# Expert-choice routing: logits in column groups of TensorE, and another place for the first weight splits

## The chip, the cores and the metric

The kernel runs on one core of a Trainium2 chip. The metric is device time of one execution in microseconds; for the kernel before, three runs were taken and their median is 1884.99 us. The core's engines are TensorE (PE, with its weight loads PEld), VectorE (DVE), ScalarE (ACT), GpSimd (POOL) and SyncE (SP), which issues most DMAs. Each engine works through its own queue in program order.

## The reference

Two layers over 1024 tokens of width 1024. Each has a mixer (layer 0: gated DeltaNet beside pooling; layer 1: a short gated convolution) with an output projection, then an expert-choice mixture of 16 experts, each of which takes the 128 tokens with the highest affinity for it. What matters here:

```
hl2 = modulate(rms_norm(xl, norm_ffn[i]), sh2_l, sc2_l)
xl = xl + g2_l[:, None] * expert_choice_ffn(hl2, router[i], w_gate[i], w_up[i], w_down[i])

def expert_choice_ffn(h, router, w_gate, w_up, w_down):
    aff = jax.nn.softmax(jnp.einsum('bnd,de->bne', h, router).astype(jnp.float32), axis=-1)
    gate, idx = lax.top_k(aff.transpose(0, 2, 1), cap)
    xg = h[bidx, idx]
    hid = jax.nn.silu(jnp.einsum('becd,edf->becf', xg, w_gate)) * jnp.einsum('becd,edf->becf', xg, w_up)
    y = jnp.einsum('becf,efd->becd', hid, w_down) * gate[..., None].astype(h.dtype)
    return jnp.zeros_like(h).at[bidx, idx].add(y)
```

## The kernel before

Large matmuls are made of three products of split operands: a float32 weight `raw` becomes `whi` (rounded to fp32r by a cast on ScalarE, L88) and `wlo` (the remainder, a subtraction at L89 on VectorE, or on GpSimd where `lo_engine` says so). Activations are split in the same way (`mh` and `ml`, `xh` and `xl`). L140 to L142 are the three products.

The output projection (`po`) goes over eight tiles of 128 tokens. As soon as half of a tile's 1024 columns is there, `route_half` transposes its four blocks (L262, `pt`), copies them (L264, `x2T`) and adds four matmuls to the tile's logits (L267, `lg`): the 128x128 block stands in the array, the router's 16 columns move through it. fp32 matmuls show as two records each, so a half has eight. `route_tile` then scales the logits (L277, `sml`), takes the softmax (L280, `sme`), transposes it into `v` (L291), and writes the modulated tile `h` and its affinities to the `table` in DRAM (L302). For tiles marked `late`, `h` is made in three steps: ScalarE's scaling (L296), then a multiplication by `a2` and an addition of `sh2` on GpSimd (L297, L300).

`select` finds the threshold of each expert by ten rounds of counting (`junk`, `cnt`, L315) with a chain of small operations between VectorE and TensorE, and then the place of each token (`before`, the tile `aff` in the rows of L356). The scratch of `select` lies in memory that the routing's pool held. `gather` turns places into indices: eight signs of 128x128 (`oh`; for the first expert four on ScalarE, L372, and four on VectorE, L370), summed on TensorE (`pi`, L373), cast to `idx` (L376), and an indirect DMA on GpSimd fetches the rows `xg` (L378). `transposed` makes `xh` and `xl` of them, and the expert's matmuls `gu` begin.

Each expert's weights are six granules of 1 MB (`granules`), which `fetch` loads into `raw` buffers, of which there are eight in the experts, and `prefetch` splits ahead of use. Up to six are split ahead. In `start0` and `start1`, four (layer 0) and six (layer 1) granules are fetched during the routing, two (layer 0) and one (layer 1) of them are split there by GpSimd and the cast, and each such split is followed by a further fetch. The rest of the six is split in `experts`: up to three on GpSimd after the last `routed` operation, the others on VectorE after `placed`, the last operation of `select`. `issue_after` sets such an order; otherwise the Tile scheduler sets it from the program and its priorities.

## Time and profile before

| what | us |
|---|---|
| runs | 1885.58, 1884.99, 1876.78 |
| profiled execution | 1877.14 |
| its span | 1875.4 |
| TensorE busy | 1667.6 (89%) |
| VectorE busy | 1288.0 (69%) |
| ScalarE busy | 898.3 (48%) |
| GpSimd busy | 518.9 (28%) |
| DMA, mean | 237 GB/s |

The span is the time from the first to the last instruction of the core, and the profiled execution is that of the rows below. A busy time says how long an engine had work in it, whether or not anything waited for it. The first routing ends near 697 us, its selection runs from 700 to 728 us, and layer 0's experts follow until some 1045 us; the second routing lies between 1376 and 1481 us, its selection ends at 1508, and the experts follow until some 1840 us.

### The profile page before, as it was taken

Reading aid. Unit: us, or ns where it says so; the run is one execution under the profiler, and the core shown is the slowest. Engines: PE = TensorE matmul, PEld = TensorE weight load, DVE = VectorE, ACT = ScalarE, POOL = GpSimd, SP = SyncE. Lnnn points to the kernel's source line nnn. Section 1 sums busy time; section 2 is a strip of 40 time slices with the busy share of each in tenths; the row PEclk is TensorE's granted clock in tenths of the full one; section 3 lists DMA queues with packets and bytes.
Section 4 is the critical chain, followed back from the end, with each engine's and each line's share of the span. In section 5 each row is a group of like instructions: output and inputs, shape, how many; then the busy total and the mean of one; then the engine's idle time right before and its main releaser. Section 6 shows DMA issues by size and latency. Waiting matters only on the chain. (4 is left out here: it accounts for less than half of the span.)

```text
span 1875.4 us, 26089 instructions
## 1 busy us (share of the span) xinstructions
PE 1667.6 (89%) x9581; PEld 1356.4 (72%) x9581; DVE 1288.0 (69%) x1964; ACT 898.3 (48%) x1568; POOL 518.9 (28%) x551
## 2 busy tenths in 40 slices
PE   5999998779979984999899899999999569999985
PEld 2998875667877773777678677888888457787774
DVE  4628685657778875789887768433545558889876
ACT  3635332433742444778766451111132367777753
POOL 4310296471431164222121261000012502211202
PEclk7989998879989985999999899999999779999998
DMA  7417665559586966899999648423264459999985
GB/s 289 146 35 228 214 203 136 158 155 280 168 295 203 386 248 211 303 341 368 363 368 324 205 131 295 163 68 109 82 222 146 175 194 330 356 373 365 362 277 190
DMA packets 261397, 443.71 MB, mean 237 GB/s; under 512 B 46521, under 2 KB 108714, under 8 KB 257174
## 3 DMA queue, kind: packets, MB, share of 16 engines
q1 hardware_dynamic: 252198, 408.76, 63.0%
q0 software_dynamic: 9072, 33.30, 7.0%
q8 instruction: 75, 1.23, 0.3%
q14 instruction: 52, 0.43, 0.1%
HBM read 368.65 MB, written 73.35 MB: 236 GB/s over the span
## 5 line engine op out<-in xcount | busy, mean ns | idle before, releaser
L89 DVE TENSOR_TENSOR wlo<-raw,whi 128x2048 fp32r<-128x2048 f32 (+3 forms) x247 | 476.4, 1960 | 91.5 <-ACT whi L88 91.4
L88 ACT CAST whi<-raw 128x2048 fp32r<-128x2048 f32 (+3 forms) x271 | 420.4, 1597 | 206.1 <-PE pin L141 67.6
L140 PE MATMUL gu<-whi,xh 128*128 128x512 f32 x512 | 207.4, 408 | 16.1 <-ACT whi L88 13.2
L141 PE MATMUL gu<-wlo,xh 128*128 128x512 f32 x512 | 207.9, 407 | 9.4 <-DVE wlo L89 9.3
L142 PE MATMUL gu<-whi,xl 128*128 128x512 f32 x512 | 204.8, 403 | 0.9 <-DVE xl L135 0.8
L484 POOL DMA_INDIRECT acc<-y,idx x31 | 72.5, 2338 | 364.6 <-DVE y L479 364.1
L141 PE MATMUL pin<-h1T,whi 128*128 128x512 f32 x384 | 149.8, 391 | 0.0
L142 PE MATMUL pin<-h1T,wlo 128*128 128x512 f32 x384 | 149.7, 392 | 0.0
L140 PE MATMUL pin<-h1T,whi 128*128 128x512 f32 x384 | 147.8, 393 | 0.0
L140 PEld LDWEIGHTS gu<-whi,xh 128*128 128x128 f32 x512 | 98.9, 194 | 42.8 <-ACT whi L88 17.5
L141 PEld LDWEIGHTS gu<-wlo,xh 128*128 128x128 f32 x512 | 98.8, 193 | 35.0 <-DVE wlo L89 12.7
L89 POOL TENSOR_TENSOR wlo<-raw,whi 128x1024 fp32r<-128x1024 f32 (+2 forms) x24 | 71.8, 3005 | 166.1 <-ACT whi L88 166.0
L142 PEld LDWEIGHTS gu<-whi,xl 128*128 128x128 f32 x512 | 98.3, 192 | 23.6 <-DVE xl L135 1.5
L810 DVE SCALAR_TENSOR_TENSOR adsum<-raw,cs,adsum 128x512 f32<-128x512 f32 (+1 forms) x77 | 95.1, 1235 | 23.5 <-DMA raw<-in_ada_w_dram 22.7
L474 PE MATMUL py<-whi,hh 128*128 128x512 f32 x256 | 106.4, 417 | 5.4 <-ACT hh L134 5.3
L474 PE MATMUL py<-wlo,hh 128*128 128x512 f32 x256 | 105.3, 411 | 0.1
L140 PE MATMUL pq<-hT,whi 128*128 128x512 f32 (+1 forms) x256 | 98.9, 386 | 3.3 <-DVE cv L1098 2.1
L378 POOL DMA_INDIRECT xg<-table,idx x32 | 49.2, 1539 | 181.3 <-ACT idx L376 148.4
L142 PE MATMUL pq<-hT,wlo 128*128 128x512 f32 (+1 forms) x256 | 98.4, 384 | 0.0
L141 PE MATMUL pq<-hT,whi 128*128 128x512 f32 (+1 forms) x256 | 98.2, 383 | 0.0
L141 PE MATMUL po<-wlo,mh 128*128 128x512 f32 x224 | 90.4, 404 | 4.7 <-DVE wlo L89 4.7
L140 PE MATMUL po<-whi,mh 128*128 128x512 f32 x224 | 90.5, 405 | 0.0
(397 smaller groups left out, 3739.1 us busy)
## 6 DMA issues: line engine op xcount, KB each, us to landing
raw<-in_w_gate_dram SPq DMA_DIRECT2D x64, 1024.0 KB
raw<-in_w_up_dram SPq DMA_DIRECT2D x64, 1024.0 KB
raw<-in_w_down_dram SPq DMA_DIRECT2D x64, 1024.0 KB
raw<-in_ada_w_dram SPq DMA_DIRECT2D x32, 1024.0 KB
raw<-in_ada_w_dram SPq DMA_DIRECT2D x64, 256.0 KB
raw<-in_sc_w_in_dram SPq DMA_DIRECT2D x12, 1024.0 KB
table<-h SPq DMA_DIRECT2D x16, 520.0 KB
raw<-in_ev_w_in_dram SPq DMA_DIRECT2D x16, 512.0 KB
```

The costliest lines, as they stand in the source:

```text
L88: nc.scalar.copy(hi[:, part], raw[:, part])
L89: (lo_engine or e).tensor_sub(lo[:, part], raw[:, part], hi[:, part])
L140: nc.tensor.matmul(out, lhs[0], rhs[0], start=start, stop=False)
L141: nc.tensor.matmul(out, lhs[0], rhs[1], start=False, stop=False)
L142: nc.tensor.matmul(out, lhs[1], rhs[0], start=False, stop=stop)
L378: nc.gpsimd.indirect_dma_start(out=xg, out_offset=None, in_=self.table[:, :], in_offset=bass.IndirectOffsetOnAxis(ap=idx, axis=0))
L474: nc.tensor.matmul(py, hh[:, k, :], g[w][:, k, :], start=k == w == 0, stop=False)
L484: self.scattered = nc.gpsimd.indirect_dma_start(out=self.acc[:, :], out_offset=bass.IndirectOffsetOnAxis(ap=idx, axis=0), in_=y, in_offset ...
L810: nc.vector.scalar_tensor_tensor(st["sum"], raw, cs[:, k, 0:1], st["sum"], op0=ALU.mult, op1=ALU.add)
```

## The change

The router's scaled columns are padded from 16 to 32 and stand in the array now, in four groups of 32 columns (`tile_position`), one for each block of 128 columns of the half; the 128 tokens move through all four. The logits come out transposed and in four partial sums on four groups of 32 partitions. When both halves are in, ScalarE copies the 128x128 partials (`lgp`) and a matmul with `fold`, a constant of four stacked identities, sums the groups and turns them back (L281 of the changed kernel). The early splits in the routing are gone, with the fetch behind each. The first round of the selection reads the constant `cand0` in place of a copy. And of the six splits ahead of the first expert, two are on GpSimd and four on VectorE, these after the last sign that VectorE makes for the first gather.

```diff
@@ -198,6 +198,11 @@
     for i, by in enumerate((-7 / 8, -1.0)):
         nc.vector.memset(co.down[:, i : i + 1], by / P)
 
+    co.fold = c.tile([P, NE], F32, name="fold")
+    nc.vector.tensor_tensor(co.fold, co.ident[:, 0:NE], co.ident[:, 32 : 32 + NE], op=ALU.add)
+    for i in (2, 3):
+        nc.vector.tensor_tensor(co.fold, co.fold, co.ident[:, 32 * i : 32 * i + NE], op=ALU.add)
+
     co.tri16 = c.tile([P, P], BF16, name="tri16")
     nc.gpsimd.memset(co.tri16, 1.0)
     nc.gpsimd.affine_select(
@@ -242,9 +247,11 @@
         nc.tensor.transpose(pt[:, : 2 * KD], rows, co.ident[: 2 * KD, : 2 * KD])
         cols = pool.tile([P, 2, KD, 1], F32, name=co.name("mod_cols"))
         nc.vector.tensor_copy(cols.rearrange("p s k o -> p (s k o)"), pt[:, : 2 * KD])
-        self.router = pool.tile([P, KD, NE], F32, name=co.name("router_a"))
+
+        self.router = pool.tile([P, KD, 32], F32, name=co.name("router_a"))
+        nc.gpsimd.memset(self.router, 0.0)
         shifts = pool.tile([P, KD, NE], F32, name=co.name("router_sh"))
-        for dst, i in ((shifts, 0), (self.router, 1)):
+        for dst, i in ((shifts, 0), (self.router[:, :, :NE], 1)):
             nc.vector.tensor_tensor(dst, w, cols[:, i].to_broadcast([P, KD, NE]), op=ALU.mult)
         pb = ps.tile([P, 512], F32, tag="y", name=co.name("pbias"))
         for k in range(KD):
@@ -262,13 +269,20 @@
             nc.tensor.transpose(pt[:, k * P : (k + 1) * P], x[:, (4 * half + k) * P : (4 * half + k + 1) * P], co.ident)
         xT = pool.tile([P, 4, P], F32, tag="x2T", name=co.name("x2T"), bufs=3)
         (nc.vector.tensor_copy if half else nc.scalar.copy)(xT.rearrange("p k t -> p (k t)"), pt)
+
         for k in range(4):
-            kk = 4 * half + k
-            nc.tensor.matmul(self.logits[:, :NE], xT[:, k, :], self.router[:, kk, :], start=kk == 0, stop=kk == KD - 1)
+            sl = slice(32 * k, 32 * k + 32)
+            nc.tensor.matmul(
+                self.logits[sl, :P], self.router[:, 4 * half + k, :], xT[:, k, :], start=half == 0, stop=half == 1, tile_position=(0, 32 * k),
+            )
+        if half:
+            parts = pool.tile([P, P], F32, tag="lgp", name=co.name("lgp"), bufs=1)
+            nc.scalar.copy(parts, self.logits[:, :P])
+            nc.tensor.matmul(self.logits[:, P : P + NE], parts, co.fold, start=True, stop=True)
 
     def route_tile(self, t, x, pool, ps, late=False):
 
-        co, nc, lg = self.co, self.nc, self.logits
+        co, nc, lg = self.co, self.nc, self.logits[:, P:]
         nc.sync.dma_start(self.acc[t * P : (t + 1) * P, :], x)
         r = co.rstd(pool, x, D, pool.tile([P, D], BF16, tag="h2j", name=co.name("h2j"), bufs=1))
 
@@ -298,7 +312,7 @@
             else:
                 nc.vector.scalar_tensor_tensor(h[:, :D], x, r, self.a2, op0=ALU.mult, op1=ALU.mult)
         self.routed = nc.gpsimd.tensor_tensor(h[:, :D], h[:, :D], self.sh2, op=ALU.add).ins
-        nc.scalar.copy(h[:, D:], e[:, 0, :])
+        self.weighed = nc.scalar.copy(h[:, D:], e[:, 0, :]).ins
         nc.sync.dma_start(self.table[t * P : (t + 1) * P, :], h)
 
     def select(self, pool, ps):
@@ -306,14 +320,13 @@
         co, nc, aff = self.co, self.nc, self.aff
         junk = pool.tile([P, SEQ], BF16, tag="junk", name=co.name("junk"), bufs=1)
         cand = pool.tile([P, 1], I32, tag="cand", name=co.name("cand"), bufs=1)
-        nc.vector.tensor_copy(cand, co.cand0)
         cnt = pool.tile([P, 1], F32, tag="cnt", name=co.name("cnt"), bufs=1)
         ok = pool.tile([P, 1], BF16, tag="ok", name=co.name("ok"), bufs=1)
         delta = pool.tile([P, 1], I32, tag="delta", name=co.name("delta"), bufs=1)
         for r in range(10):
-            step = 2.0 ** (27 - 3 * r)
+            step, old = 2.0 ** (27 - 3 * r), cand if r else co.cand0
             nc.vector.tensor_scalar(
-                junk, self.v, cand.bitcast(F32), 0.0, op0=ALU.is_ge, op1=ALU.add, accum_out=cnt
+                junk, self.v, old.bitcast(F32), 0.0, op0=ALU.is_ge, op1=ALU.add, accum_out=cnt
             )
             nc.vector.tensor_scalar(ok, cnt, float(CAP), None, op0=ALU.is_ge)
             pn = ps.tile([P, 512], F32, tag="tr", name=co.name("pn"))
@@ -321,7 +334,7 @@
             nc.tensor.matmul(pn[:, :1], co.same, ok, start=False, stop=True)
             if r < 7:
 
-                nc.vector.scalar_tensor_tensor(cand, pn[:, :1], step, cand, op0=ALU.mult, op1=ALU.add)
+                nc.vector.scalar_tensor_tensor(cand, pn[:, :1], step, old, op0=ALU.mult, op1=ALU.add)
             else:
                 nc.vector.tensor_scalar(delta, pn[:, :1], step, None, op0=ALU.mult)
                 nc.vector.tensor_tensor(cand, cand, delta, op=ALU.add)
@@ -353,9 +366,9 @@
 
         self.before = aff
         flat = lambda t: t.rearrange("p t e -> p (t e)")
-        self.placed = nc.vector.scalar_tensor_tensor(
+        nc.vector.scalar_tensor_tensor(
             flat(self.before), pp[:, : NT * NE], -1.0, flat(equal), op0=ALU.mult, op1=ALU.subtract
-        ).ins
+        )
 
     def gather(self, e, pool, ps, shared=False):
 
@@ -367,7 +380,7 @@
             before, vector = self.before[:, t, e : e + 1], int(shared and t % 2)
             if vector:
 
-                nc.vector.tensor_scalar(oh[:, t, :], co.places, before, 0.0, op0=ALU.add, op1=ALU.is_gt)
+                self.shared = nc.vector.tensor_scalar(oh[:, t, :], co.places, before, 0.0, op0=ALU.add, op1=ALU.is_gt).ins
             else:
                 nc.scalar.activation(oh[:, t, :], co.places, AF.Sign, bias=before)
             nc.tensor.matmul(pi[:, :1], oh[:, t, :], co.ones16[:, vector : vector + 1], start=t == 0, stop=t == NT - 1)
@@ -433,10 +446,10 @@
             with co.tc.issue_after(self.numbered):
                 rows.append(self.gather(e, pool, ps))
         ahead = self.transposed(rows[0][2], pool, ps)
-        with co.tc.issue_after(self.routed):
-            self.prefetch(weights, min(3, 6 - len(self.ahead)), nc.gpsimd)
-        with co.tc.issue_after(self.placed):
-            self.prefetch(weights, 6 - len(self.ahead), nc.vector)
+        with co.tc.issue_after(self.routed), co.tc.issue_after(self.weighed):
+            self.prefetch(weights, 2, nc.gpsimd)
+            with co.tc.issue_after(self.shared):
+                self.prefetch(weights, 4, nc.vector)
         for e in range(NE):
             (idx, aff, _), halves = rows.pop(0), ahead
             if e + 3 < NE:
@@ -1781,7 +1794,7 @@
 
     def start0(make, wpb, pool, ps, _):
         moe = make()
-        early = Weights(co, raws, Cycle(*((p, 1) for p in wpb)))
+        early = Weights(co, raws, wpa)
         ada = ada_steps(1, 0, pool, raws, ps, "tr")
         x_pool = Cycle((Bufs(out_pool, 3), 3), (Bufs(pool, 2), 2))
         for i, (t, srcs) in enumerate(pass2.items()):
@@ -1789,9 +1802,6 @@
                 step()
             if i == 4:
                 moe.fetch(early, 4)
-            if i in (5, 6):
-                moe.prefetch(early, 1, nc.gpsimd)
-                moe.fetch(early, 1)
             for step in out_project(
                 co, t, lambda: split_tile(co, out_pool, srcs), ws, part, out_pool, ps,
                 lambda t, x, late=i > 5: moe.route_tile(t, x, pool, ps, late), lambda t, x, nh: moe.route_half(t, x, nh, pool, ps), x_pool=x_pool,
@@ -1848,9 +1858,6 @@
         for i, steps in enumerate(tiles):
             if i == 1:
                 moe[0].fetch(weights, 6)
-            if i == 4:
-                moe[0].prefetch(weights, 1, nc.gpsimd)
-                moe[0].fetch(weights, 1)
             for step in steps:
                 step()
         return moe[0]
```

The order of VectorE at the end of layer 0's selection, before (`equal` and `aff` are its last two operations, `oh` the signs, `xl` the low half of the first expert's rows):

```order
L356 SCALAR_TENSOR_TENSOR aff_6918<-pp_7760,equal_7780 128x128
L89 TENSOR_TENSOR wlo_7891<-raw_7480,whi_7890 128x2048
L370 TENSOR_SCALAR oh_7788<-places,aff_6918 128x128 x4
L135 TENSOR_TENSOR xl_7866<-pt_7860,xh_7865 128x512
L135 TENSOR_TENSOR xl_7875<-pt_7869,xh_7874 128x512
L89 TENSOR_TENSOR wlo_8075<-raw_8072,whi_8074 128x2048
```

and with the change:

```order
L369 SCALAR_TENSOR_TENSOR aff_6923<-pp_7772,equal_7792 128x128
L383 TENSOR_SCALAR oh_7800<-places,aff_6923 128x128 x4
L89 TENSOR_TENSOR wlo_7899<-raw_7311,whi_7898 128x2048
L89 TENSOR_TENSOR wlo_7903<-raw_7313,whi_7902 128x2048
L89 TENSOR_TENSOR wlo_7909<-raw_7906,whi_7908 128x2048
L89 TENSOR_TENSOR wlo_7915<-raw_7912,whi_7914 128x2048
L135 TENSOR_TENSOR xl_7878<-pt_7872,xh_7877 128x512
```

The signs have moved ahead of the splits, and there are four splits where there was one.

The order of ScalarE from the last tile of layer 0's routing to the first signs, before:

```order
L296 ACTIVATE h_7648<-ox_7576,rstd_7631 128x1024
L292 COPY aff_6918<-sme_7639 128x16
L301 COPY h_7648<-sme_7639 128x16
L88 CAST whi_7886<-raw_7388 128x2048
L88 CAST whi_7890<-raw_7480 128x2048
L372 ACTIVATE oh_7788<-places,aff_6918 128x128 x4
L376 ACTIVATE idx_7806<-pi_7789 128x1
```

and with the change:

```order
L310 ACTIVATE h_7661<-ox_7586,rstd_7644 128x1024
L306 COPY aff_6923<-sme_7652 128x16
L315 COPY h_7661<-sme_7652 128x16
L88 CAST whi_7890<-raw_7307 128x2048
L88 CAST whi_7894<-raw_7309 128x2048
L88 CAST whi_7908<-raw_7906 128x2048
L88 CAST whi_7914<-raw_7912 128x2048
L88 CAST whi_7898<-raw_7311 128x2048
L88 CAST whi_7902<-raw_7313 128x2048
L385 ACTIVATE oh_7800<-places,aff_6923 128x128 x4
L389 ACTIVATE idx_7818<-pi_7801 128x1
```

Six casts, in place of two, stand between the last tile and the signs.

The order of GpSimd at the same place (L300 and L314 are the addition of `sh2`, L297 and L311 the multiplication by `a2`), before:

```order
L300 TENSOR_TENSOR h_7377<-h_7377,bc_6890 128x1024
L156 TENSOR_TENSOR rstd_7631<-rstd_7631,mhalf 128x1
L300 TENSOR_TENSOR h_7469<-h_7469,bc_6890 128x1024
L297 TENSOR_TENSOR h_7562<-h_7562,bc_6888 128x1024
L297 TENSOR_TENSOR h_7648<-h_7648,bc_6888 128x1024
L300 TENSOR_TENSOR h_7562<-h_7562,bc_6890 128x1024
L300 TENSOR_TENSOR h_7648<-h_7648,bc_6890 128x1024
L89 TENSOR_TENSOR wlo_7879<-raw_7294,whi_7878 128x2048
L89 TENSOR_TENSOR wlo_7883<-raw_7296,whi_7882 128x2048
L89 TENSOR_TENSOR wlo_7887<-raw_7388,whi_7886 128x2048
```

and with the change:

```order
L314 TENSOR_TENSOR h_7397<-h_7397,bc_6894 128x1024
L314 TENSOR_TENSOR h_7484<-h_7484,bc_6894 128x1024
L156 TENSOR_TENSOR rstd_7644<-rstd_7644,mhalf 128x1
L311 TENSOR_TENSOR h_7572<-h_7572,bc_6892 128x1024
L314 TENSOR_TENSOR h_7572<-h_7572,bc_6894 128x1024
L311 TENSOR_TENSOR h_7661<-h_7661,bc_6892 128x1024
L314 TENSOR_TENSOR h_7661<-h_7661,bc_6894 128x1024
L89 TENSOR_TENSOR wlo_7891<-raw_7307,whi_7890 128x2048
L89 TENSOR_TENSOR wlo_7895<-raw_7309,whi_7894 128x2048
L391 DMA xg_7821<-table_73,idx_7818 128x1040
```

An addition stands now between the two last multiplications, and two splits follow where there were three.

## Rows read from the trace of the kernel before

**Rows 1.** Windows; columns: us, busy us PE, PEld, DVE, ACT, POOL, PEclk, DMA share, GB/s.

```profile
740.00:760.00 20.00, 20.00 (x94) 16.31 (x93) 11.66 (x10) 17.36 (x30) 1.61 (x2) 0.92 0.56 178
860.00:920.00 60.00, 56.03 (x271) 44.67 (x270) 50.33 (x37) 45.82 (x64) 12.17 (x7) 0.97 1.05 362
...
1430.00:1450.00 20.00, 20.00 (x103) 16.65 (x104) 12.09 (x19) 7.08 (x18) 5.36 (x3) 1.00 0.33 107
```

**Rows 2.** Chain of waits, second routing: start us, us, what; one such row of nine.

```profile
1429.31 0.80 PE lg L267 x8
```

**Rows 3.** Timeline of TensorE, second routing: start us, us, engine, line, operation, operands.

```profile
1428.69 0.39 PE L142 MATMUL po<-whi,ml 128*128 128x512 f32 x1
1428.92 0.39 PE L140 MATMUL po<-whi,mh 128*128 128x512 f32 x1
...
1429.95 0.48 PE L141 MATMUL po<-wlo,mh 128*128 128x512 f32 x1
1430.27 0.39 PE L142 MATMUL po<-whi,ml 128*128 128x512 f32 x1
```

**Rows 4.** Timeline of TensorE, column groups of the adaLN reduction.

```profile
670.38 1.07 PE L818 MATMUL pad<-adsum,ones 128*32 128x512 f32 x8
671.37 0.66 PE L262 MATMUL pt<-ident,ox 128*128 128x128 f32 x4
```

**Rows 5.** Timeline, end of the first routing; in brackets: idle before, releaser.

```profile
693.24 2.35 POOL L300 TENSOR_TENSOR h<-h,bc 128x1024 f32<-128x1024 f32 x1 [2.43 <-DVE sm L283]
695.54 4.65 POOL L297 TENSOR_TENSOR h<-h,bc 128x1024 f32<-128x1024 f32 x2
...
700.22 0.15 DVE L309 COPY cand<-cand 128x1 int32<-128x1 int32 x1 [3.29 <-POOL h L297]
```

**Rows 6.** Timeline, end of the second routing, ScalarE and VectorE.

```profile
1474.88 1.90 ACT L88 CAST whi<-raw 128x2048 fp32r<-128x2048 f32 x1 [0.94 <-PE po L142]
...
1481.30 0.14 DVE L309 COPY cand<-cand 128x1 int32<-128x1 int32 x1
```

**Rows 7.** Timeline behind the first selection.

```profile
727.78 0.29 DVE L356 SCALAR_TENSOR_TENSOR aff<-pp,equal 128x128 f32<-128x128 f32 x1
727.99 2.28 DVE L89 TENSOR_TENSOR wlo<-raw,whi 128x2048 fp32r<-128x2048 f32 x1
...
730.19 0.73 DVE L370 TENSOR_SCALAR oh<-places,aff 128x128 f16<-128x128 f16 x4
...
731.21 0.17 ACT L376 ACTIVATE idx<-pi 128x1 int32<-128x1 f32 x1 [1.82 <-PE pi L373]
...
739.44 0.69 DVE L135 TENSOR_TENSOR xl<-pt,xh 128x512 fp32r<-128x512 f32 x1 [8.51 <-ACT xh L134]
...
739.46 0.79 PE L140 MATMUL gu<-whi,xh 128*128 128x512 f32 x1 [1.43 <-ACT xh L134]
```

**Rows 8.** Timeline behind the second selection.

```profile
1507.35 0.29 DVE L356 SCALAR_TENSOR_TENSOR aff<-pp,equal 128x128 f32<-128x128 f32 x1
1507.56 4.48 DVE L89 TENSOR_TENSOR wlo<-raw,whi 128x2048 fp32r<-128x2048 f32 x2
...
1512.97 0.17 ACT L376 ACTIVATE idx<-pi 128x1 int32<-128x1 f32 x1 [4.02 <-PE pi L373]
...
1523.31 0.80 PE L140 MATMUL gu<-whi,xh 128*128 128x512 f32 x1 [1.40 <-ACT xh L134]
...
1534.67 0.37 SPq L71 DMA_DIRECT2D raw<-in_w_gate_dram  x1
```

**Rows 9.** Timeline of ScalarE, last casts within the two selections.

```profile
713.76 3.70 ACT L88 CAST whi<-raw 128x2048 fp32r<-128x2048 f32 x2 [16.45 <-POOL wlo L89]
...
1490.10 1.90 ACT L88 CAST whi<-raw 128x2048 fp32r<-128x2048 f32 x1 [8.33 <-DMA table<-h]
```

**Rows 10.** Timeline of SyncE's queue, first and last of 13 granule loads, layer 0.

```profile
631.77 0.38 SPq L71 DMA_DIRECT2D raw<-in_w_gate_dram  x1
...
720.26 0.37 SPq L71 DMA_DIRECT2D raw<-in_w_gate_dram  x1
```


## The prediction

> **What bounds the kernel now.** I read the page's first part, then the windows of the stages around the change, then the timelines of the two routings and of the two moments after a selection, and last the chain of waits over the second routing. TensorE is busy 89% of the span, but that is a mean over stages of three kinds, and the windows separate them [rows 1]. In the out-projection with its routing it is busy for all 20.00 us of a 20 us window at full clock (1430 to 1450), with DMA at 0.33: there whatever TensorE no longer executes comes off the time. In the experts (860 to 920) TensorE is at 56.03 of 60 us while the DMA share is 1.05: two engines are both close to their bound, so an earlier start counts only if loads and matmuls both begin earlier. Between them lies the selection, a serial chain on VectorE, and behind it the stretch in which the first expert's rows are numbered and gathered. There TensorE waits, and each microsecond of delay is a microsecond of the kernel. In the window 740 to 760 the DMA share is only 0.56, so loads have room just behind the selection.
>
> **Part 1, logits in column groups.** The chain of waits carries the logits of a half tile at 0.80 us [rows 2], one such row for nearly every half. The timeline agrees: the projection's matmul at 1428.92 is followed by the next at 1429.95, 1.03 us later, where neighbours without logits stand 0.23 apart (as 1428.69 and 1428.92 do) and this one's successor follows after 0.32 [rows 3]. So a half costs 1.03 - 0.23 = 0.80 and a break of 0.32 - 0.23 = 0.09, together 0.89 us. The new form is four groups of 32 columns with 128 moving columns, eight records in place of eight. The only rows with such groups are the adaLN reductions: eight records of 512 moving columns, four groups of 32, hold TensorE from 670.38 to 671.37, 0.99 us [rows 4]. If all of it scaled with the columns, 128 of them would cost 0.99 / 4 = 0.25; if none did, 0.99. I take 0.36 and the same break of 0.09, so 0.45 a half, as much nearer the lower end as eight records that overlap should be (alone, eight records of 512 columns at the 0.23 spacing of rows 3 would need 1.84 us, so the 0.99 shows that groups do overlap). That saves 0.44 a half. Each tile now pays a fold: two records of a matmul with 16 columns, 2 x 0.10 (0.80 / 8) and a break, 0.29, taken as 0.3.
>
> Layer 1: the order has 14 halves ahead of the last projection matmul before and after, and 6 folds now. 14 x 0.44 - 6 x 0.3 = 4.4 us saved. Layer 0: the scheduler had 11 halves ahead of it, and has 13 with 6 folds and one more group of four transposes (estimate 0.35 to 0.5): 11 x 0.89 - 13 x 0.45 - 6 x 0.3 - 0.4 = 1.8 us saved.
>
> One rule speaks against this. The Trainium skill, TensorEngine Tiling (Array Packing), Key Properties, says that a change of tiling mode, not just of tile, drains the TensorE; here the mode changes twice a half tile. The row of the groups [rows 4] shows no drain as a gap, since the next operation starts at 671.37 while the last group ends at 671.45, but it cannot exclude one inside the 0.99. By the rule the half would lie nearer the upper end, which is rival B.
>
> **Part 2, the tail of the routing.** In layer 0 the selection does not wait for its data but for GpSimd: the copy of the candidates at 700.22 waited 3.29 us for the second of the two multiplications that fill 695.54 to 700.19 [rows 5]. The first count inherits that wait. The order of GpSimd now has the addition for h_7572 ahead of the last multiplication, one operation of 2.33 us more (4.65 / 2). Against it stands the idle time of 2.43 us ahead of 693.24 [rows 5], which an earlier tile can fill. The ends are -2.3 and +2.3; I take +0.1. In layer 1 a weight cast of 1.90 us at 1474.88 stands ahead of the last tile's square on ScalarE and is gone; the last tile gains a copy and a fold on its chain, and the order has the modulation of the tile before it ahead of its scaling on VectorE [rows 6]. Ends: -1.9, the cast alone, and as much the other way, since nothing in the rows prices the two additions together; I take +0.9, because copy and fold are certain and the cast's end, 1476.78, left the square only part of its length to wait. The early splits of the routing (two granules in layer 0, one in layer 1) cost nothing on TensorE, whose queue was full beside them; their removal is put at nothing.
>
> **Part 3, the copy of candidates.** 0.14 us at 1481.30 and 0.15 at 700.22 [rows 5, 6], each on the serial chain, with the gap behind each 0.2 (estimate): 0.4 us saved.
>
> **Part 4, behind the selection.** Let t be the end of the last operation of the selection, 728.07 and 1507.64 [rows 7, 8]. In layer 0 the split at 727.99 keeps VectorE from its four signs until 730.19, so the index is ready at 731.21, t + 3.1. In layer 1 two splits, 4.48 us, do the same and the index comes at 1512.97, t + 5.3. After the change VectorE's signs (0.73) come first and are done before ScalarE's four, which end at t + 1.3; the 0.3 us that TensorE and ScalarE need from the last sign to the index (730.92 to 731.21) put it at t + 1.6. So 1.5 us are won in layer 0. In layer 1 the index alone gives 3.7, and up to 2.1 more: the first expert's matmul came 8.25 us behind the index in layer 0 but 10.34 in layer 1 (1523.31), where two loads were issued right at the gather. I take 5.0 there. Four splits of 2.28 now lie behind the signs, 9.1 us, and end at about t + 10.0; VectorE was idle there for 8.51 and, in layer 1, as long, and its next work, the low half xl, is first needed a few matmuls into the first expert. If this cover were short, the xl would cost the 1 us by which it is late.
>
> What ScalarE has to do is the other condition: six casts of 1.90 us, 11.4 us, stand now ahead of its signs on a queue that keeps its order. Before, the cast at 713.76 waited 16.45 us, by the row for GpSimd's splits, and that at 1490.10 waited 8.33 for the table's write [rows 9]; the fifth and sixth of the six take this place now, behind two GpSimd splits too. If they are let go at the same moments, they end 3.8 us later, near 717.6 and 1493.9, and are covered by 10 and 13 us of selection. Nothing is charged.
>
> **Sum.** Layer 0: -1.8 + 0.1 - 0.2 - 1.5 = -3.4. Layer 1: -4.4 + 0.9 - 0.2 - 5.0 = -8.7. Together -12.1 us, against the profiled execution's own 1877.1: 1865.0. The median of the three runs, 1885.0, lies 7.9 above that execution, so the forecast for a median is **1872.9**. About 0.5%, 9.4 us, is what a measurement of this kernel can tell from no change.
>
> **Rivals.** *B, the groups do not pay.* With 0.99 + 0.09 a half, 0.63 above what I took, 27 halves lose 17 us: 1889.9, no change. For it: the drain, and that eight records of 16 columns already cost only 0.10 each, hardly more than a group's own overhead. Against it: 0.99 was paid for four times the columns. *C, the experts swallow the earlier start.* The DMA share of 1.05 in them says that if loads end the stage, the 6.5 us of part 4 are lost and 5.6 stay: 1879.4, no change. Against it: the load behind the seventh split goes out at 1534.67, t + 27.0 [rows 8], and would now go out once the first granule is used, 10 us (gather and casts) plus 7.6 (twelve matmuls at the 0.63 us of the cold clock seen there) and the split, t + 20. *D, slower: the load stream starts further behind.* Before, 13 loads were out by t in layer 0 (631.77 to 720.26 [rows 10]) and 12 in layer 1 by the same count; now four raw buffers come free only from t + 3 to t + 10, so ten are out. If DMA bounds the experts all through, three and two loads of 1.05 MB at about 360 GB/s, 2.9 us each, come on top: 14.5 - 5.6 = 8.9 us slower, 1893.9, and a loss of 1 us in part 2 takes it over 0.5%. It decides if the fifteenth load is issued no earlier than before (t + 27.0 in layer 1). Against it is the 0.56 of window 740 to 760 [rows 1]: there is room to make three loads good. *E, the casts hold the signs.* If the two granules loaded only now, the table's write or GpSimd's splits let the casts go over 10 us later than before [rows 9], part 4 turns round, us for us.
>
> **Chances.** Forecast 0.60; B 0.13; C 0.15; D 0.08; E 0.04. The forecast's own range is 1862 to 1880, from the ends of the group price (0.25 saves 3 us more, 0.6 costs 6), of the GpSimd order and of which level the runs fall in. With B and C the range goes to 1890. Faster by over 0.5% needs a time under 1875.6: most of the forecast, a little of C, 0.54. Within 0.5%: the rest of it, B and C, 0.37. Slower: 0.09, from D and E.
>
> **What would show it.** Right: in the layer 1 routing the spacing around a half's logits falls from 1.03 to about 0.6; the last projection matmul of that pass comes some 4 us sooner counted from its first; the index stands at t + 1.6 in both layers; the first expert's matmul at about t + 10. Wrong: a half's logits at 0.8 or more (B); the first count later behind the last projection matmul than the 14 and 7 us of before by over 2 (part 2); waits for weights in the experts up by several us while the DMA share stays at 1.05 (C, D); ScalarE's first sign waiting for a cast rather than for the selection (E).

## The result and the profile after

Slower. Eleven runs of the changed kernel have a median of 1893.21 us (1888.84 to 1898.06), eleven of the kernel before 1882.60 (1876.78 to 1888.72): a ratio of 1.0061 [1.0045, 1.0077], where 1872.9 (1862 to 1890) was forecast. Ratios here and below stand with their 95% interval and are not the quotients of the medians. The profiled execution took 1892.96 us, its span 1891.0 (before 1877.14 and 1875.4).

The page of the profile after: engines, busy us, share of the span and instructions.

```profile
PE 1657.4 (88%) x9613; PEld 1333.4 (71%) x9613; DVE 1278.7 (68%) x1970; ACT 900.4 (48%) x1581; POOL 532.3 (28%) x545
```

TensorE has 10 us less to do, VectorE 9, and yet the end is later: time is lost in waiting. A table by stage, from the timelines of both profiled executions, shows where (t is the end of the selection's last operation; the last down-projection is the start of its last eight matmuls, the products with `hl`):

| stage, us | layer 0: before, after | layer 1: before, after |
|---|---|---|
| first to last projection matmul | 125.58, 125.29 | 111.97, 106.32 |
| last projection matmul to first count | 13.86, 12.93 | 7.03, 7.30 |
| first count to t | 27.66, 23.40 | 26.16, 23.40 |
| t to first expert matmul | 11.39, 19.10 | 15.67, 19.45 |
| first expert matmul to last down-projection | 322.2, 327.5 | 320.9, 326.1 |

Layer 1's pass and both selections gain; all of it and more is lost behind t. The rows add up to 8.4 of the 15.6 us between the two spans. Of the rest 3.6 lie ahead of the first projection matmul (560.97 before, 564.56 after) and 2.8 between layer 0's last down-projection (1061.70 and 1072.79, so layer 0's experts end near 1064 before, not near 1045) and layer 1's first projection, stretches that the change hardly touches; the medians differ by 10.6. Timeline of the changed kernel behind the first selection, which answers to [rows 7]:

```profile
725.89 0.29 DVE L369 SCALAR_TENSOR_TENSOR aff<-pp,equal 128x128 f32<-128x128 f32 x1
...
726.22 0.74 DVE L383 TENSOR_SCALAR oh<-places,aff 128x128 f16<-128x128 f16 x4
...
726.88 8.89 DVE L89 TENSOR_TENSOR wlo<-raw,whi 128x2048 fp32r<-128x2048 f32 x4
...
727.80 0.17 ACT L389 ACTIVATE idx<-pi 128x1 int32<-128x1 f32 x1 [0.31 <-PE pi L386]
...
728.88 7.98 POOL L391 DMA_INDIRECT xg<-table,idx  x1 [14.75 <-ACT oh L385]
...
743.49 1.12 PE L404 MATMUL pt<-ident,xg 128*128 128x128 f32 x4 [12.20 <-DMA xg<-table,idx]
...
745.28 0.79 PE L140 MATMUL gu<-whi,xh 128*128 128x512 f32 x1 [0.51 <-ACT xh L134]
```

The index is there at 727.80, as early as forecast (t + 1.6). But the gather, which GpSimd starts at 728.88, takes **7.98 us**; before, the same gather took 1.22. It ends at 736.86, 1.09 after the last of VectorE's four splits (726.88 + 8.89 = 735.77), and TensorE waits 12.20 for its rows. Layer 1 repeats it [rows 8]:

```profile
1513.08 0.29 DVE L369 SCALAR_TENSOR_TENSOR aff<-pp,equal 128x128 f32<-128x128 f32 x1
...
1514.06 8.89 DVE L89 TENSOR_TENSOR wlo<-raw,whi 128x2048 fp32r<-128x2048 f32 x4
...
1514.99 0.17 ACT L389 ACTIVATE idx<-pi 128x1 int32<-128x1 f32 x1 [0.31 <-PE pi L386]
...
1515.44 8.44 POOL L391 DMA_INDIRECT xg<-table,idx  x1 [11.42 <-ACT oh L385]
...
1532.82 0.79 PE L140 MATMUL gu<-whi,xh 128*128 128x512 f32 x1 [0.51 <-ACT xh L134]
...
1544.15 0.37 SPq L71 DMA_DIRECT2D raw<-in_w_gate_dram  x1
```

8.44 us for the gather (1.05 before), its end 0.93 behind that of the splits (1522.95). The fifteenth load goes out at t + 30.8, where t + 20 was forecast.

### The profile page after: what moved, and what is told of

Read it like the earlier page. It is cut to its first block, busy times and chain, and to the rows that moved or that the text cites. A ratio compares the mean times of both kernels' runs of the same rounds, so it can differ in the third digit from the quotient of the medians.

```text
span 1891.0 us, 26180 instructions
## 1 busy us (share of the span) xinstructions
PE 1657.4 (88%) x9613; PEld 1333.4 (71%) x9613; DVE 1278.7 (68%) x1970; ACT 900.4 (48%) x1581; POOL 532.3 (28%) x545
## 4 chain that ended last, share of the span: by engine, by line
PE 46%; DVE 10%; DMA 10%; issue 7%; ACT 4%; POOL 1%; SPq 1%; DVEq 0%; ACTq 0%; POOLq 0%
PE py L487 4%; PE gu L142 4%; PE gu L141 4%; PE pin L140 4%; PE gu L140 4%; PE pin L141 4%; PE pin L142 4%; PE po L141 3%; PE po L142 3%; PE po L140 3%; DMA xg<-table,idx 3%; DVE wlo L89 2%; ACT whi L88 2%; PE py L490 2%; DVE junk L328 1%
## 5 line engine op out<-in xcount | busy, mean ns | idle before, releaser
L89 DVE TENSOR_TENSOR wlo<-raw,whi 128x2048 fp32r<-128x2048 f32 (+3 forms) x252 | 487.1, 1968 | 108.6 <-ACT whi L88 108.4
L497 POOL DMA_INDIRECT acc<-y,idx x31 | 83.2, 2685 | 321.2 <-DVE y L492 319.4
L391 POOL DMA_INDIRECT xg<-table,idx x32 | 75.6, 2364 | 192.8 <-ACT idx L389 163.0
L89 POOL TENSOR_TENSOR wlo<-raw,whi 128x1024 fp32r<-128x1024 f32 (+2 forms) x16 | 48.3, 3072 | 152.4 <-ACT whi L88 152.2
```

Source lines behind the costliest of these rows:

```text
L89: (lo_engine or e).tensor_sub(lo[:, part], raw[:, part], hi[:, part])
L391: nc.gpsimd.indirect_dma_start(out=xg, out_offset=None, in_=self.table[:, :], in_offset=bass.IndirectOffsetOnAxis(ap=idx, axis=0))
L497: self.scattered = nc.gpsimd.indirect_dma_start(out=self.acc[:, :], out_offset=bass.IndirectOffsetOnAxis(ap=idx, axis=0), in_=y, in_offset ...
```

## The experiments

Theory G: VectorE's back-to-back subtractions, which read two operands from SBUF (the on-chip memory of the kernel's ordinary tiles; matmuls write to another, PSUM), keep GpSimd from issuing the gather. Rivals: the loads that the splits release (L), the loads' later start (rival D of the prediction), and the groups (B).

**1. Before, with four more subtractions behind the signs, no loads.** The last split's subtraction is repeated, with the same values.

```diff
+        with co.tc.issue_after(self.shared):
+            for _ in range(4):
+                nc.vector.tensor_sub(*weights.last)
```

> The kernel before, with the last of its split subtractions repeated four times on VectorE right behind its four signs of the first gather; no load is added. Theory (VectorE's subtractions with two SBUF inputs keep GpSimd from making the first gather's descriptors): the first gather takes about 9 us in both layers in place of 1.22 and 1.05 and ends about 1 us behind the last repeated subtraction; the first expert's matmul moves from t + 11.4 and t + 15.7 to about t + 19 and t + 23. Rival (the four loads that follow the four splits compete with the gather): nothing is loaded here, so the gather stays under 1.5 us and the first expert's matmul within 1 us of before, except for the low half xl.

Neither came. The kernel took 1879.0 in its one execution, before 1886.64 on the same chip; the gathers took 1.94 and 2.39, and the first matmuls came at t + 11.6 and t + 13.6. But the repeats write the same tile, so each waits for the one ahead: four take 9.26 where those of the change take 8.89. The gather got in at the first such pause. The experiment had not built what it meant to test; run 9 mends it.

**2 and 3. The change, with its splits behind the first gather.** VectorE waits for a one-element GpSimd memset that stands behind the gather. Run 3 holds the last two splits until behind the first `xl` as well.

```diff
+        with co.tc.issue_after(self.gathered):
+            nc.gpsimd.memset(mark[:, 0:1], 0.0)
+        with co.tc.issue_after(self.shared):
+            marked = nc.vector.tensor_copy(mark[:, 1:2], mark[:, 0:1]).ins
...
-            with co.tc.issue_after(self.shared):
+            with co.tc.issue_after(marked):
```

> The changed kernel, with the four VectorE splits held until GpSimd has issued the first gather (a one-element memset on GpSimd behind the gather, which VectorE copies ahead of the splits). Theory: the first gather takes 0.95 to 1.3 us in place of 7.98 and 8.44, the first expert's matmul comes at about t + 10 to t + 11 in place of t + 19.1 and t + 19.5, its first xl some 2 us late behind the splits; 12 to 16 us off the whole time, so 1877 to 1881. Rival (loads compete): the loads come only some 2 us later than in the changed kernel, so the matmul stays behind t + 16 and the time within 6 us of the changed kernel.

> As the run before, but only two of the four VectorE splits stand between the first gather and the first expert's xl, two behind it. Theory: gather and first matmul as there, the wait for xl gone, so 0 to 4 us less than there. Rival (the load stream sets the experts' end): two raw buffers come free 5 us later than there, and the time is the same or up to 5 us more.

Run 2: 1882.16, 0.9957 [0.993, 0.9984] of before; run 3: 1879.34, 0.9965 [0.9941, 0.999]. In both the gathers take 1.22 and 1.06, as in before, and the first matmul stands at t + 9.86 in both layers, what the forecast had (t + 10). So about 1% of the changed kernel's time hangs on the place of the splits. Part of the earlier start is lost in the experts: from the first matmul they take 340.6 and 322.3 in run 2, 335.5 and 330.5 in run 3.

**4. The groups alone.** Before, with column groups and without the copy of the candidates; all splits as before.

```diff
+            nc.tensor.matmul(
+                self.logits[sl, :P], self.router[:, 4 * half + k, :], xT[:, k, :], start=half == 0, stop=half == 1, tile_position=(0, 32 * k),
+            )
```

> The kernel before with the column groups, the fold and the removed copy of candidates alone; splits and loads as before. Theory (the groups pay about what was forecast): 0.36 to 0.45 us a half in place of 0.89, the second out-projection 4 to 6 us shorter, 5 to 9 us off the time of before. Rival (groups do not overlap or drain): halves at 0.8 or more, time as before or above.

1871.06, 0.9902 [0.9865, 0.9939], and layer 1's pass at 106.21: rival B falls. The selections take 25.8 and 26.2 us, where the change takes 23.4, so the gain there is not the copy's.

**5. The change once more,** with the same code.

> The changed kernel once more, unaltered, as the reference of the runs that stand beside it. Every theory expects the first gather at about 8 us in both layers, the first expert's matmul at t + 19 to t + 20, and a ratio to the kernel before of about 1.006.

1894.99, 1.0060 [1.0033, 1.0088]; gathers 7.98 and 8.44.

**6. Before, with later loads.** Granule loads from the eleventh on wait for the end of the selection: ten are out by t, as in the change. This is one half of rival D's condition; the other, that the next four wait for buffers, is not built (they go out at t + 0.4 to t + 4.4, in the change at t + 3.0 to t + 9.6).

```diff
+            if self.count > 10:
+                with self.co.tc.issue_after(self.held):
+                    self.fetched.append(weights.fetch(next(self.stream), (4, 512)))
```

> The kernel before, with its granule loads from the eleventh on held until the selection has ended (a small DMA on SyncE's queue that waits for the last operation of the selection stands ahead of them): ten loads are out by t, as in the changed kernel, in place of 13 and 12. Splits, signs and the first gather are as before. Theory (the load stream bounds the experts from t on, rival D of the prediction): the experts, counted from t to the last down projection, get 6 to 9 us longer in layer 0 (three loads of 2.9 us) and 4 to 6 in layer 1, 10 to 15 us in all. Rival (there is room for the loads just behind t): less than 3 us in all, unless the first gather itself gets longer.

1885.47, 1.0010 [0.9983, 1.0036]: D's 10 us and more do not appear. The gather itself took 1.22, its rows then came late behind the released loads (first matmul at t + 19.05 and t + 19.08, as late as in the change), and yet layer 0's experts, at 314.4 us from their first matmul, made it good: from t to the last down-projection it took 333.5, before 333.6 (layer 1: 339.9 and 336.5). A late first matmul need not cost its full length where the loads run on meanwhile.

**7 and 10. The change with pauses.** Behind each of the four splits VectorE copies one element of that split's result. The splits, their engine, the loads and the order on every other engine stay.

```diff
+            after = self.shared
+            for i in range(4):
+                with co.tc.issue_after(after):
+                    self.prefetch(weights, 1, nc.vector)
+                    after = nc.vector.tensor_copy(gap[:, i : i + 1], self.ahead[-1][1][:, 3, 511:512]).ins
```

> The changed kernel, with a one-element copy behind each of the first three VectorE splits that reads the split's own result, so that VectorE pauses for a moment between splits; loads follow the splits as in the changed kernel, under 1 us later. Theory (GpSimd gets its way only in a pause between VectorE's operations, and the four splits run without one): the first gather takes 1.5 to 3 us in place of 8, the first expert's matmul comes at t + 11 to t + 14, 5 to 12 us off the changed kernel. Rival (the four loads beside it hold the gather): the gather stays at 7 to 9 us.

> The changed kernel with the one-element copies between its splits once more, unaltered, as the reference of the run beside it: about 0.5% below the kernel before.

1873.26, 0.9948 [0.9917, 0.998], and the second time 1873.27, 0.9945 [0.9927, 0.9964]. Timeline behind the first selection of run 7:

```profile
722.21 2.28 DVE L89 TENSOR_TENSOR wlo<-raw,whi 128x2048 fp32r<-128x2048 f32 x1
...
724.21 1.38 POOL L391 DMA_INDIRECT xg<-table,idx  x1 [14.74 <-ACT oh L385]
...
724.53 0.15 DVE L456 CAST gap<-wlo 128x1 fp32r<-128x1 f32 x1
...
724.61 2.29 DVE L89 TENSOR_TENSOR wlo<-raw,whi 128x2048 fp32r<-128x2048 f32 x1
...
732.73 0.79 PE L140 MATMUL gu<-whi,xh 128*128 128x512 f32 x1 [0.51 <-ACT xh L134]
```

The pause between 724.49 and 724.61 is enough: the gather that started at 724.21 takes 1.38, and the first matmul comes at t + 11.2 (t is 721.52). More work on VectorE, and 21.7 us less than run 5 on the same chip (1894.99). L falls: the loads are the same, at t + 3.0 to t + 10.2 (in the change to t + 9.6). Of the 18.4 us between the two profiled spans (1891.0 and 1872.6), 6.6 and 6.9 lie between t and the last down-projection of the two layers; 4.7 lie ahead of the first selection's end, where both programs issue the same, 4.5 of them already ahead of the first projection matmul (564.56 and 560.08).

**8 and 11. The early splits kept.** Groups, no copy, the routing's early splits as before, two on GpSimd in the selection; what is missing to six granules behind the gather (run 8) or with the pauses of run 7 (run 11). The lines compare with the kernel before.

```diff
-            self.prefetch(weights, min(3, 6 - len(self.ahead)), nc.gpsimd)
+            self.prefetch(weights, 2, nc.gpsimd)
```

> The column groups and the removed copy, with the early splits and fetches in the routing as in the kernel before, two splits on GpSimd within the selection and the remaining two (layer 0) and three (layer 1) on VectorE behind the first gather. If both causes hold (gather held by VectorE, load stream behind): the selection is 23.4 us in both layers, the first matmul at t + 10, 12 and 11 loads out by t, and it is the fastest of all, 1 to 8 us below the column groups alone, near 1865 to 1870 where the kernel before is at 1886. If only the gather counted, it is equal to the run with all four VectorE splits behind the gather.

> The changed kernel with those copies, and with the early splits and fetches in the routing given back (two granules in layer 0, one in layer 1), so two and three splits on VectorE behind the signs in place of four. Theory (without the early splits the experts run some 5 us a layer longer, since fewer loads are out when the selection ends): 5 to 12 us less than the run beside it, near 0.99 of the kernel before. Rival (the early splits cost or bring nothing): within 3 us of the run beside it.

Run 8: 1868.50, 0.9896 [0.9834, 0.9958]; run 11: 1869.42, 0.9923 [0.9905, 0.994]. Run 11 lies 3.9 us under run 10 on the same chip, less than expected. Both selections take 23.4 us. These two and run 4 are the best versions, about 1% under the kernel before, and can't be told from one another.

The profiles show that those 3.9 us are what is left of a gain and a loss. From t to the last down-projection run 11 takes 4.3 and 4.4 us less than run 10. All other kernels whose first gather is not held agree: the two layers together take 665 to 673 us there with the early splits and the loads behind them (before, runs 1, 4, 6, 8, 11), 679 to 686 without (runs 2, 3, 7, 10). But layer 0's routing takes 5.8 longer in run 11, from the mixer's last matmul to the last projection matmul 85.95 against 80.14. Run 4 shows why, in its timeline of layer 0's pass, GpSimd's early split beside VectorE's split of `mix`:

```profile
637.83 0.43 DVE L135 TENSOR_TENSOR ml<-mix,mh 128x256 fp32r<-128x256 f32 x1 [1.31 <-ACT mh L134]
...
648.72 5.15 POOL L89 TENSOR_TENSOR wlo<-raw,whi 128x1024 fp32r<-128x1024 f32 x2 [4.75 <-ACT whi L88]
...
649.07 2.61 DVE L135 TENSOR_TENSOR ml<-mix,mh 128x256 fp32r<-128x256 f32 x1
...
655.22 0.80 PE L140 MATMUL po<-whi,mh 128*128 128x512 f32 x1 [4.24 <-DVE ox L649]
```

Beside GpSimd's split an operation of 0.43 takes 2.61, and TensorE waits 4.24. Runs 8 and 11 have the same (2.60 and waits of 4.22 and 4.23), the kernel before has not. So the early splits would be worth more than 3.9 us if GpSimd did them where VectorE has no operation with two SBUF operands in a chain; no run here tries that.

**9. Before, with sixteen quarter subtractions without a pause.** Run 1 made right: each repeat writes another quarter of the tile than the one ahead, with the same values as before, and nothing is loaded.

```diff
+            for i in range(16):
+                q = i % 4
+                nc.vector.tensor_sub(*(t[:, q] for t in weights.last))
```

> As the first run (the kernel before with repeated subtractions behind VectorE's signs and no further load), but in sixteen quarters of 128x512 that take turns over the four quarters of the split, so that none depends on the one just ahead of it and VectorE has no pause between them. Theory (GpSimd gets its way only in a pause between VectorE's operations with two SBUF inputs): the first gather takes 7 to 10 us in both layers and ends about 1 us behind the last subtraction, where it took 1.94 and 2.39 us beside four subtractions that wait for each other; the first expert's matmul moves to t + 17 or later in layer 0. Rival (it was the loads behind the splits in the changed kernel after all): the gather stays under 2.5 us.

1904.04 in its one execution, beside 1883.16. Timeline behind its first selection:

```profile
733.63 9.72 DVE L444 TENSOR_TENSOR wlo<-raw,whi 128x512 fp32r<-128x512 f32 x16
...
735.06 9.37 POOL L379 DMA_INDIRECT xg<-table,idx  x1 [12.05 <-ACT oh L373]
```

The gather takes 9.37 us (9.82 in layer 1) and ends 1.08 behind the last of the sixteen (743.35). No load, no group and no moved split is in this kernel: the subtractions alone hold the gather. Theory G stands.

## Why the prediction was wrong

**The step that failed** is the cover of part 4: "Four splits of 2.28 now lie behind the signs, 9.1 us [...] VectorE was idle there for 8.51". The splits were priced by the engine that runs them. Idle on VectorE was not free: GpSimd needed a moment without them just then. The forecast had the first matmul at t + 10; it came at t + 19.10 and t + 19.45, 18.5 us too late together, and run 2, whose splits wait for the gather, shows the forecast's place (t + 9.86). The waiting list of after names the wait as "PE pt L404 <- DMA xg<-table,idx" (24.8 us in two), and the busy time of GpSimd even rises, from 518.9 to 532.3: what tells that GpSimd is being held is the mean length of a gather, 1.54 us before and 2.36 after.

**A second term failed beside it.** Part 2 says of the early splits: "their removal is put at nothing". Where they stood they cost next to nothing (80.4 us of layer 0's pass before, 80.0 after, see below), but without them and the loads behind them the experts run longer: 5.3 and 5.2 us from the first expert matmul in the change, and run 11, which gives them back to run 10, wins 4.3 and 4.4 from t on. Whether it is the splits, the loads, or the fewer splits that are then left behind t, is open.

The evidence was in the trace of before. Timeline of before, the gathers of layer 0's fourth and of a later expert, and the splits beside the latter:

```profile
743.35 0.94 POOL L378 DMA_INDIRECT xg<-table,idx  x1 [2.68 <-ACT idx L376]
...
838.19 6.69 DVE L89 TENSOR_TENSOR wlo<-raw,whi 128x2048 fp32r<-128x2048 f32 x3
...
841.12 4.61 POOL L378 DMA_INDIRECT xg<-table,idx  x1 [1.98 <-ACT idx L376]
```

With no split beside it a gather takes 0.94; with three back to back it takes 4.61 and ends at 845.73, 0.85 behind them (844.88; VectorE goes on there without a pause, with `hl<-pt,hh`, one operand of which lies in PSUM). I read only the first gathers, which ran while VectorE was idle. The Trainium skill, SBUF — State Buffer, SBUF: two separate sides, has a part of this: the ports that VectorE and GpSimd share are locked for a whole instruction, by a VectorE operation with two SBUF inputs only against a GpSimd operation that reads SBUF. As what starves a DMA from GpSimd's queue of its descriptors it names VectorE operations in a 2-port perf mode, and not subtractions such as these. The trace agrees that one of the two waits (7.98 against 1.22), and it goes further than the page: here plain subtractions hold a gather, and the first one past three boundaries between splits, in run 9 past many, until they broke off.

**Selection, forecast at nothing, measured -4.3 and -2.8: luck.** (The copy of part 3 stands ahead of the first count and so in the tails below.) The gain is the same conflict the other way round, which the forecast did not know. Timelines of before, around round 8's integer addition in each selection:

```profile
715.73 4.50 POOL L89 TENSOR_TENSOR wlo<-raw,whi 128x2048 fp32r<-128x2048 f32 x1 [2.02 <-ACT whi L88]
...
715.82 4.43 DVE L327 CUSTOM_DVE_ANT_0 cand<-cand,delta 128x2 uint16<-128x2 uint16 x1
...
1486.37 13.43 POOL L89 TENSOR_TENSOR wlo<-raw,whi 128x2048 fp32r<-128x2048 f32 x3
...
1496.89 2.92 DVE L327 CUSTOM_DVE_ANT_0 cand<-cand,delta 128x2 uint16<-128x2 uint16 x1
```

and of the changed kernel in the first:

```profile
718.20 0.16 DVE L340 CUSTOM_DVE_ANT_0 cand<-cand,delta 128x2 uint16<-128x2 uint16 x1
```

The addition of two columns took 4.43 and 2.92 and ended with GpSimd's third split (720.25 against 720.23, 1499.81 against 1499.80); with two splits GpSimd is done at 714.13, ahead of it, and it takes 0.16, as in before's rounds 9 and 10. Part 4 let GpSimd's splits lie beside the selection without asking what they hold.

**Part 1, groups: right.** TensorE's timeline of the changed kernel, second routing [rows 3]:

```profile
1465.97 0.39 PE L141 MATMUL po<-wlo,mh 128*128 128x512 f32 x1
...
1466.29 0.43 PE L275 MATMUL lg<-x2T,router_a 128*32 128x128 f32 x8
...
1466.65 0.50 PE L142 MATMUL po<-whi,ml 128*128 128x512 f32 x1
...
1466.99 0.40 PE L140 MATMUL po<-whi,mh 128*128 128x512 f32 x1
...
1470.65 0.40 PE L142 MATMUL po<-whi,ml 128*128 128x512 f32 x1
...
1470.89 0.29 PE L281 MATMUL lg<-fold,lgp 128*128 128x16 f32 x2
...
1471.03 0.47 PE L140 MATMUL po<-whi,mh 128*128 128x512 f32 x1
...
1471.34 0.40 PE L141 MATMUL po<-wlo,mh 128*128 128x512 f32 x1
```

A half costs (0.68 - 0.23) + (0.34 - 0.23) = 0.56 (forecast 0.45), a fold (0.38 - 0.23) + (0.31 - 0.23) = 0.23 (forecast 0.3). 14 x (0.89 - 0.56) - 6 x 0.23 = 3.2; layer 1's pass fell 5.7 (forecast 4.4, so the total came near it with the unit prices too low). For the rest the rows offer the clock at its start. TensorE's timeline of before has there 32 records of 16 columns, bias and first logits:

```profile
1381.72 1.85 PE L251 MATMUL pbias<-router_sh,ones 128*128 128x16 f32 x16
...
1383.42 2.12 PE L267 MATMUL lg<-router_a,x2T 128*128 128x16 f32 x16
```

and its window 1380 to 1390 a granted clock of 0.83 (columns as in [rows 1]):

```profile
1380.00:1390.00 10.00, 10.00 (x57) 8.92 (x56) 3.16 (x8) 2.69 (x7) 0.00 (x0) 0.83 0.20 60
```

The window of after at the same distance from its first projection matmul (17.6 us) has 1.00:

```profile
1394.00:1404.00 10.00, 10.00 (x76) 8.21 (x75) 2.88 (x7) 3.46 (x6) 0.00 (x0) 1.00 0.25 76
```

A clock of 0.83 for 10 us is some 1.7 us of work not done at full speed (of its two levels, the lower one for a third of the window); the same stretch has 0.83, 0.83 and 0.71 in runs 1, 9 and 6, without groups, and 1.00 in runs 2, 4, 5 and 7, with them. That the records of 16 columns brought it down was not tried by itself, and 0.8 us stay unexplained. A drain (rival B), if there is one, lies within the 0.45 of the half itself, under the 0.80 of the old form.

**Layer 0's pass, forecast -1.8 (its terms give -1.7): not to be told.** Its projections begin while the mixer still runs on TensorE, so the mixer's last matmul is the better start. From there to the last projection matmul before takes 80.4 us, runs 1, 6 and 9, whose routing is the same, 80.9 to 81.7. The change and runs 2, 3, 5, 7 and 10, alike there too, take 80.0 to 81.8. The two groups of profiles overlap, and the term is lost in their spread. The 86 and 87 of runs 4, 8 and 11 are the conflict shown above.

**Part 2, tails.** -0.9 and +0.3 where, with the copy of part 3, -0.1 and +0.7 were forecast. In layer 0 the first count still waits for GpSimd. Timeline of after:

```profile
700.39 2.35 POOL L311 TENSOR_TENSOR h<-h,bc 128x1024 f32<-128x1024 f32 x1
...
702.78 1.28 DVE L328 TENSOR_SCALAR_CACHE_REDUCE junk<-v,cand 128x1024 bf16<-128x1024 f32 x1 [4.86 <-POOL h L311]
...
726.22 1.28 ACT L385 ACTIVATE oh<-places,aff 128x128 f16<-128x128 f16 x4 [10.75 <-DVE aff L369]
```

**Rivals.** E did not happen: ScalarE's first sign waited 10.75 for the selection (`aff`), no cast stood in its way. D and C are in part what the experts show: in the change, and in runs 2, 3, 7, they take from 322 to 341 us from their first matmul, before 322.2 and 320.9. D's sign came, the fifteenth load at t + 30.8, but mostly because the gather was held: in run 2 it goes out at t + 22.3 and t + 20.3. (The forecast's t + 20 took 0.63 us a matmul; that is the length of one record, and they start 0.43 apart.) That D's 1893.9 lies next to the measured 1893.21 is luck: D had 14.5 us from the loads alone, where run 6 shows 3.2 for ten loads by t; 13.5 lie between run 7 and the change from t on, where the loads are the same, and the selections gave back 7.0 that D did not have.

## What to carry to other kernels

A gap on one engine is not free room if the work put there shares a path with an engine on the critical chain: for VectorE work with two SBUF operands ask what GpSimd issues beside it, for GpSimd elementwise work what two-operand steps VectorE has in a serial chain. Look in the trace for one operation at several lengths (a gather at 0.94 and at 4.61) and at what ran beside the long ones; if the two must meet, put the long operations behind the gather's issue, or leave a pause among them. And price a removal like an addition: ask what else hung on the work that goes.

## What the runs showed of the hardware

- A GpSimd gather of 128 rows took 0.94 to 1.22 us alone and 7.98 to 9.82 beside VectorE subtractions of two SBUF operands without pauses (four of 2.28, or sixteen quarters). A one-element copy that depends on the split let it in (1.38, 1.83). What lets a gather in without a pause is open: in run 2's layer 0 the second and third gather got in at the first boundary between the same four splits (2.40 and 1.49).
- In the other direction a VectorE integer addition of two columns was held 4.43 and 2.92 us by a GpSimd split of 4.5, and took 0.16 without it; a VectorE split of 256 columns took 2.61 beside a GpSimd split and 0.43 without.
- Eight records of 128 columns in four groups of 32 cost 0.45 us and a break of 0.11, where eight of 16 columns had cost 0.80 and 0.09.
